# A dilated 3x3 convolution: the tile framework's streams replaced by hand-written ones, with a loop on TensorE

## The chip, the cores and the metric

The kernel runs on one core of a Trainium2 chip. The metric is the device time of one execution in microseconds (us). A core has TensorE (PE in the profile; PEld is its weight loads), VectorE (DVE), ScalarE (ACT), GpSimd (POOL) and SyncE (SP). Here SP issues every transfer, and 16 DMA engines carry them.

## The reference

```python
batch, c_in, h, w, c_out, k, dilation = 16, 64, 64, 64, 128, 3, 2
x_pad = np.pad(x, ((0, 0), (0, 0), (2, 2), (2, 2)))
for b, co, ci, kh, kw:   # five nested loops
    output[b, co] += weight[co, ci, kh, kw] * x_pad[b, ci, 2*kh : 2*kh + h, 2*kw : 2*kw + w]
```

Everything is float32: the input is 16 images of 64 channels and 64x64 pixels (16.8 MB), the output 16 images of 128 channels (33.6 MB).

## The kernel before

**Tiling.** Two images stand side by side on the 128 partitions (64 channels each), so there are 8 pairs. A pair is cut into 4 groups of 16 rows: 32 groups, numbered G. A matmul multiplies the 64 channels of one image with one tap; the two images use the upper and the lower half of the rows of TensorE's array, so their matmuls stand in twos that run side by side.

**Arithmetic.** The vertical taps are rearranged so that 5 products replace 6 per two output rows. ScalarE casts a pair's chunk to 16 bits (`cast`, L74). VectorE adds rows that lie two apart (`rowsum`, L86). TensorE makes three sums in PSUM for each group: psP from the row sums (weights of kind 0, 6 matmuls), psA (kinds 1 and 2, 12 matmuls) and psB (kinds 3 and 4, 12 matmuls), all at L172. ScalarE copies psP to SBUF (`p_sb`, L234). VectorE adds p_sb to psA and to psB and writes two rows of the output in turn (L241). psP has one buffer of two PSUM banks, psA and psB share three.

**Head.** SP loads the weights (L89) and then x (L65): pair 0 in two parts, pair 1, pair 2. The weights are combined into the 5 kinds on VectorE, ScalarE and GpSimd (L112 to L116) and turned by matmuls with an identity (L125), with dummy matmuls (L102) between.

**Order of the work.** The kernel is written in the order in which each engine is to work, inside `tc.manual_schedule()`; the tile framework places the waits. Every matmul of all 32 groups is an instruction of its own, with a weight load ahead of it. For each group the order is: products (P, A, B; in group 0 A, B, P), copy of psP, up to two casts for later groups (`casts`), the row sum of the next group, the two additions. SP's queue holds loads and stores in one fixed order (end of the loop over G): after pair 0's halves come `store_both` (L192) and the loads of pairs 3 and 4, after pairs 1 and 2 `store` (L186) mixed with the loads of pairs 5, 6 and 7, and then stores alone. x has three float32 buffers, the output three (each two images, 4.2 MB). The transfers' completions are counted on eight semaphores used in turn, so that a transfer also waits for the one eight before it.

**End.** The last pair is stored in halves. The last 8 rows of one first half (`ROWS4`, `FOUR`) are split into 124 partitions and 4 partitions. The second halves of the last two images (1 MB each) go out after group 31. L310 is the end of the program, which waits for all transfers and lets the engines meet.

Of the kernel before, what the change touches and what calls it, by code (L numbers as in the profile page):

```python
# [10 lines left out]
def kernel(  # L11
# [7 lines left out]
    nc = tc.nc  # L19
# [5 lines left out]
    assert B % 2 == 0  # L25
# [15 lines left out]
    ngroups = npairs * NG  # L41
    chunk_rows = [(g * GR + (d if g else 0), min((g + 1) * GR + d, H)) for g in range(NG)]
    XF = 3

    wpool = ctx.enter_context(tc.tile_pool(name="wpool", bufs=1))
    fpool = ctx.enter_context(tc.tile_pool(name="fpool", bufs=XF))
    xpool = ctx.enter_context(tc.tile_pool(name="xpool", bufs=3))
    sxpool = ctx.enter_context(tc.tile_pool(name="sxpool", bufs=2))
    opool = ctx.enter_context(tc.tile_pool(name="opool", bufs=3))
    spool = ctx.enter_context(tc.tile_pool(name="spool", bufs=3))  # L50
    ppool = ctx.enter_context(tc.tile_pool(name="ppool", bufs=1, space=bass.MemoryType.PSUM))
    apool = ctx.enter_context(tc.tile_pool(name="apool", bufs=3, space=bass.MemoryType.PSUM))
# [4 lines left out]
    ctx.enter_context(tc.manual_schedule())  # L57

    x32_tiles, x16_tiles, xs_tiles, o_tiles = {}, {}, {}, {}

    def load(pb, cuts=(0, H)):
        if pb not in x32_tiles:
            x32_tiles[pb] = fpool.tile([P, HW], f32, tag="x32", name="x32")
        for lo, hi in zip(cuts[:-1], cuts[1:]):
            nc.sync.dma_start(  # L65
                out=x32_tiles[pb][:, lo * W : hi * W], in_=x_pair[pb, :, lo * W : hi * W]
            )

    def cast(c):
        pb, g = divmod(c, NG)  # L70
        lo, hi = chunk_rows[g]
        if g == 0:
            x16_tiles[pb] = xpool.tile([P, HW], f16, tag="x16", name="x16")
        nc.scalar.copy(  # L74
            out=x16_tiles[pb][:, lo * W : hi * W], in_=x32_tiles[pb][:, lo * W : hi * W]
        )

    def rowsum(c):
        pb, g = divmod(c, NG)
        if g == 0:  # L80
            xs_tiles[pb] = sxpool.tile([P, HW // 2], f16, tag="xs", name="xs")
        v = x16_tiles[pb][:, g * GR * W : (g + 1) * GR * W].rearrange(
            "p (b e q) -> p b e q", e=2, q=2 * W
        )
        s = xs_tiles[pb][:, g * NH : (g + 1) * NH].rearrange("p (b q) -> p b q", q=2 * W)
        nc.vector.tensor_tensor(out=s, in0=v[:, :, 0], in1=v[:, :, 1], op=add)  # L86

    w32 = wpool.tile([CO, CI * KH * KW], f32, name="w32")
    nc.sync.dma_start(out=w32, in_=weight.rearrange("o i h w -> o (i h w)"))  # L89
    load(0, (0, 2 * GR + d, H))  # L90
    load(1)
    load(2)
    zero = wpool.tile([P, 512], f16, name="zero")
    nc.vector.memset(zero, 0.0)  # L94
    ident = wpool.tile([P, P], f16, name="ident")
    make_identity(nc, ident)

    dm = ppool.tile([P, 2 * NH], f32, tag="p", name="dm")

    def dummies(n):  # L100
        for _ in range(n):
            nc.tensor.matmul(out=dm[:, 0:512], lhsT=zero[:, 0:P], rhs=zero)  # L102

    KINDS = 5
    NT = KINDS * KW
    wd = wpool.tile([CO, NT * CI], f16, name="wd")
    wdv = wd.rearrange("o (k j i) -> o k j i", k=KINDS, j=KW)
    wv = w32.rearrange("o (i h w) -> o h w i", h=KH, w=KW)
    w_sb = wpool.tile([P, NT * CO], f16, name="w_sb")

    dummies(8)
    nc.vector.tensor_copy(out=wdv[:, 0], in_=wv[:, 1])  # L112
    nc.gpsimd.tensor_tensor(out=wdv[:, 3], in0=wv[:, 0], in1=wv[:, 1], op=sub)  # L113
    nc.scalar.copy(out=wdv[:, 2], in_=wv[:, 0])  # L114
    nc.vector.tensor_tensor(out=wdv[:, 1], in0=wv[:, 2], in1=wv[:, 1], op=sub)
    nc.gpsimd.tensor_copy(out=wdv[:, 4], in_=wv[:, 2])  # L116

    wts = [apool.tile([P, 1024], f32, tag="ab", name="wt") for _ in range(3)]

    def turn(k):  # L120
        c0 = k // 3 * 512
        for j in range(KW):
            t = k * KW + j
            for r in range(2):
                nc.tensor.matmul(  # L125
                    out=wts[k % 3][r * CI : (r + 1) * CI, c0 + j * CO : c0 + (j + 1) * CO],
                    lhsT=wd[:, t * CI : (t + 1) * CI],
                    rhs=ident,
                )
        return w_sb[:, k * KW * CO : (k + 1) * KW * CO], wts[k % 3][:, c0 : c0 + KW * CO]  # L130

    x16_tiles[0] = xpool.tile([P, HW], f16, tag="x16", name="x16")
    t0 = turn(0)
    dummies(2)
    nc.vector.tensor_copy(out=t0[0], in_=t0[1])  # L135
    t1 = turn(1)
    nc.scalar.copy(out=t1[0], in_=t1[1])  # L137
    t2 = turn(2)
    nc.vector.tensor_copy(out=t2[0], in_=t2[1])  # L139
    dummies(1)  # L140
    t3 = turn(3)
    t4 = turn(4)
    dummies(1)
    nc.vector.tensor_copy(
        out=x16_tiles[0][:, 8 * W : 18 * W], in_=x32_tiles[0][:, 8 * W : 18 * W]
    )
    nc.scalar.copy(out=x16_tiles[0][:, 0 : 8 * W], in_=x32_tiles[0][:, 0 : 8 * W])
    nc.scalar.copy(out=t3[0], in_=t3[1])
    nc.vector.tensor_copy(out=t4[0], in_=t4[1])
    rowsum(0)  # L150

    ahead = [1]

    def casts(G):
        for n in range(2 if G else 3):
            c = ahead[0]
            if c >= ngroups or c > G + (7 if c < 2 * NG else 5):
                return
            cast(c)
            ahead[0] += 1  # L160

    def product(ps, src, kind, blk0, nblk, first, last):
        for j in (1, 0, 2):
            dw = (j - 1) * d
            o0, o1 = max(0, -dw), W - max(0, dw)
            t = kind * KW + j
            for hb in range(2):
                pp = slice(hb * CI, (hb + 1) * CI)
                rhs = src(pp, dw + o0, dw + o1)
                po = ps[:, hb * NH + blk0 * 2 * W : hb * NH + (blk0 + nblk) * 2 * W]  # L170
                po = po.rearrange("p (r w) -> p r w", w=W)[:, :, o0:o1]
                nc.tensor.matmul(  # L172
                    out=po,
                    lhsT=w_sb[pp, t * CO : (t + 1) * CO],
                    rhs=rhs,
                    start=first and j == 1,
                    stop=last and j == 2,
                )

    def blocks(x16, b0, n, e):  # L180
        v = x16.rearrange("p (b e r w) -> p b e r w", e=2, r=2, w=W)
        return lambda pp, c0, c1: v[pp, b0 : b0 + n, e, :, c0:c1]

    def store(pb, m, r0=0, r1=H, rows=((0, P),)):
        for lo, hi in rows:
            nc.sync.dma_start(  # L186
                out=out_img[2 * pb + m, lo:hi, r0 * W : r1 * W],
                in_=o_tiles[pb][lo:hi, m * HW + r0 * W : m * HW + r1 * W],
            )

    def store_both(pb, r0, r1):
        nc.sync.dma_start(  # L192
            out=out_img[2 * pb : 2 * pb + 2, :, r0 * W : r1 * W].rearrange("m o q -> o m q"),
            in_=o_tiles[pb].rearrange("p (m q) -> p m q", m=2)[:, :, r0 * W : r1 * W],
        )

    FOUR = ((0, P - 4), (P - 4, P))
    ROWS4 = 8

    for G in range(ngroups):  # L200
        pb, g = divmod(G, NG)
        x16 = x16_tiles[pb]
        xs = xs_tiles[pb].rearrange("p (r w) -> p r w", w=W)
        if g == 0:
            o_tiles[pb] = opool.tile([P, 2 * HW], f32, tag="osb", name="osb")
        o = o_tiles[pb].rearrange("p (m b e q) -> p m b e q", m=2, e=2, q=2 * W)
        b0 = g * NBLK

        def summed():
            ps = ppool.tile([P, 2 * NH], f32, tag="p", name="psP")  # L210
            sv = lambda pp, c0, c1: xs[pp, g * GR // 2 : (g + 1) * GR // 2, c0:c1]
            product(ps, sv, 0, 0, NBLK, True, True)
            return ps

        if G:
            psP = summed()

        psA = apool.tile([P, 2 * NH], f32, tag="ab", name="psA")
        product(psA, blocks(x16, b0, NBLK, 1), 1, 0, NBLK, True, False)
        z = 1 if g == 0 else 0  # L220
        product(psA, blocks(x16, b0 + z - 1, NBLK - z, 1), 2, z, NBLK - z, False, True)

        psB = apool.tile([P, 2 * NH], f32, tag="ab", name="psB")
        product(psB, blocks(x16, b0, NBLK, 0), 3, 0, NBLK, True, False)
# [3 lines left out]
        if not G:  # L228
            psP = summed()
# [85 lines left out]
```

## Time and profile before

| | |
|---|---|
| device time, median of 3 runs (lowest to highest) | 126.77 us (126.62 to 127.77) |
| the profiled execution: its span, first to last instruction | 125.0 us |
| median above that span | 1.8 us |
| TensorE busy | 105.8 us in 2004 instructions (1002 matmuls, 1002 weight loads) |
| VectorE, ScalarE, GpSimd busy | 91.0, 64.9, 2.2 us |
| bytes moved | 50.8 MB, mean 406 GB/s |

The profile gives the span of the profiled execution, and no separate device time of it; the 1.8 us are counted as lying around the span. A line of the waits says which engine waited for whom, how long in total, how often and the longest. In a timeline each row has the start, the length, engine, line and tiles. A row of the table by stretches has the busy time of the engines, the granted clock, the share of the 16 DMA engines' time in use and the GB/s moved.

### The profile page before, as it was taken

Reading aid. Unit: us, or ns where it says so; the run is one execution under the profiler, and the core shown is the slowest. Engines: PE = TensorE matmul, PEld = TensorE weight load, DVE = VectorE, ACT = ScalarE, POOL = GpSimd, SP = SyncE. Lnnn points to the kernel's source line nnn. Section 1 sums busy time; section 2 is a strip of 40 time slices with the busy share of each in tenths; the row PEclk is TensorE's granted clock in tenths of the full one; section 3 lists DMA queues with packets and bytes.
Section 4 is the critical chain, followed back from the end, with each engine's and each line's share of the span. In section 5 each row is a group of like instructions: output and inputs, shape, how many; then the busy total and the mean of one; then the engine's idle time right before and its main releaser. Section 6 shows DMA issues by size and latency. Waiting matters only on the chain.

```text
span 125.0 us, 2343 instructions
## 1 busy us (share of the span) xinstructions
PE 105.8 (85%) x1002; PEld 57.0 (46%) x1002; DVE 91.0 (73%) x103; ACT 64.9 (52%) x68; POOL 2.2 (2%) x8
## 2 busy tenths in 40 slices
PE   6996999999999999999999999999999999600000
PEld 2353555555555555555555555555555555200000
DVE  0561998988898889888988898889888988700000
ACT  4188896665666566656665666566653333100000
POOL 2400000000000000000000000000000000000000
PEclk9999999999999999999999999999999999985555
DMA  5999999999999999999999999999999999999991
GB/s 142 368 450 435 430 401 315 430 422 420 443 427 435 412 441 438 401 435 435 425 430 427 420 435 430 435 420 435 420 430 430 430 425 435 430 414 412 420 395 73
DMA packets 4722, 50.78 MB, mean 406 GB/s; under 512 B 488, under 2 KB 488, under 8 KB 1000
## 3 DMA queue, kind: packets, MB, share of 16 engines
q1 hardware_dynamic: 4712, 50.63, 96.7%
q8 instruction: 8, 0.13, 0.4%
q14 instruction: 2, 0.02, 0.0%
HBM read 17.07 MB, written 33.55 MB: 405 GB/s over the span
## 4 chain that ended last, share of the span: by engine, by line
PE 76%; DMA 6%; ACT 2%; DVE 1%; DVEq 1%; SPq 1%; issue 0%
PE psA L172 31%; PE psB L172 30%; PE psP L172 16%; DMA x<-in_x_dram 6%; ACT x L74 2%; DVE osb L241 1%; DVEq L310 1%; ACT p_sb L234 1%; SPq L65 0%; SPq L89 0%; DVEq L241 0%
## 5 line engine op out<-in xcount | busy, mean ns | idle before, releaser
L172 PEld LDWEIGHTS <-w_sb 64*128 64x128 f16 x960 | 54.6, 94 | 45.8 <-issue 1.4
L234 ACT COPY p_sb<-psP 128x1024 f32<-128x1024 f32 x32 | 32.4, 1012 | 36.9 <-issue 21.5
L241 DVE TENSOR_TENSOR osb<-psA,p_sb 128x1024 f32<-128x1024 f32 x32 | 39.2, 1225 | 13.4 <-PE psA L172 9.8
L172 PE MATMUL psA<-x,w_sb 64*128 64x496 f16 (+3 forms) x384 | 45.1, 365 | 0.0
L172 PE MATMUL psB<-x,w_sb 64*128 64x496 f16 (+3 forms) x384 | 45.1, 365 | 0.0
L241 DVE TENSOR_TENSOR osb<-psB,p_sb 128x1024 f32<-128x1024 f32 x32 | 39.1, 1222 | 0.0
L74 ACT CAST x<-x 128x1024 f16<-128x1024 f32 (+2 forms) x31 | 32.1, 1044 | 0.5 <-DMA x<-in_x_dram 0.3
L172 PE MATMUL psP<-xs,w_sb 64*128 64x496 f16 (+1 forms) x192 | 26.0, 371 | 1.1 <-ACT p_sb L234 1.1
L86 DVE TENSOR_TENSOR xs<-x 128x512 f16<-128x512 f16 x32 | 13.3, 416 | 0.4 <-ACT x L74 0.4
L102 PE MATMUL dm<-zero 128*128 128x512 f16 x12 | 5.3, 579 | 1.2 <-DVE zero L94 1.2
L102 PEld LDWEIGHTS <-zero 128*128 128x128 f16 x12 | 1.4, 128 | 3.2 <-issue 1.8
L112 DVE CAST wd<-w 128x192 f16<-128x192 f32 x1 | 0.5, 503 | 2.4 <-DMA w<-in_weight_dram 2.4
L125 PEld LDWEIGHTS <-wd 128*64 128x64 f16 x30 | 1.0, 118 | 1.8 <-DVE wd L112 0.8
L137 ACT CAST w_sb<-wt 128x384 f16<-128x384 f32 x1 | 0.5, 478 | 2.3 <-PE wt L125 2.3
L114 ACT ACT_TABLE_LOAD x1 | 1.3, 1283 | 0.7 <-PEq L296 0.7
L125 PE MATMUL wt<-ident,wd 128*64 128x128 f16 x30 | 1.6, 241 | 0.0
L114 ACT CAST wd<-w 128x192 f16<-128x192 f32 x1 | 0.5, 539 | 1.5 <-DMA w<-in_weight_dram 1.5
L139 DVE CAST w_sb<-wt 128x384 f16<-128x384 f32 x1 | 0.6, 557 | 0.7 <-PE wt L125 0.7
L135 DVE CAST w_sb<-wt 128x384 f16<-128x384 f32 x1 | 0.6, 558 | 0.5 <-PE wt L125 0.5
L94 DVE MEMSET zero<- 128x256 uint32 x1 | 0.3, 272 | 0.9 <-PEq L296 0.9
L113 POOL TENSOR_TENSOR wd<-w 128x192 f16<-128x192 f32 x1 | 0.8, 799 | 2.3 <-DMA w<-in_weight_dram 2.3
L116 POOL CAST wd<-w 128x192 f16<-128x192 f32 x1 | 0.8, 806 | 0.0
(11 smaller groups left out, 3.8 us busy)
## 6 DMA issues: line engine op xcount, KB each, us to landing
out_dram<-osb SPq DMA_DIRECT2D x13, 2048.0 KB, 14.9
x<-in_x_dram SPq DMA_DIRECT2D x6, 2048.0 KB, 17.0
out_dram<-osb SPq DMA_DIRECT2D x5, 1024.0 KB, 13.1
x<-in_x_dram SPq DMA_DIRECT2D x2, 1024.0 KB, 13.2
x<-in_x_dram SPq DMA_DIRECT2D x1, 1088.0 KB, 5.6
x<-in_x_dram SPq DMA_DIRECT2D x1, 960.0 KB, 7.4
out_dram<-osb SPq DMA_DIRECT2D x1, 768.0 KB, 15.4
w<-in_weight_dram SPq DMA_DIRECT2D x1, 288.0 KB, 2.8
```

The source lines that it names most:

```text
L74: nc.scalar.copy(out=x16_tiles[pb][:, lo * W : hi * W], in_=x32_tiles[pb][:, lo * W : hi * W])
L86: nc.vector.tensor_tensor(out=s, in0=v[:, :, 0], in1=v[:, :, 1], op=add)
L102: nc.tensor.matmul(out=dm[:, 0:512], lhsT=zero[:, 0:P], rhs=zero)
L113: nc.gpsimd.tensor_tensor(out=wdv[:, 3], in0=wv[:, 0], in1=wv[:, 1], op=sub)
L114: nc.scalar.copy(out=wdv[:, 2], in_=wv[:, 0])
L116: nc.gpsimd.tensor_copy(out=wdv[:, 4], in_=wv[:, 2])
L125: nc.tensor.matmul(out=wts[k % 3][r * CI : (r + 1) * CI, c0 + j * CO : c0 + (j + 1) * CO], lhsT=wd[:, t * CI : (t + 1) * CI], rhs=ident,)
L135: nc.vector.tensor_copy(out=t0[0], in_=t0[1])
L172: nc.tensor.matmul(out=po, lhsT=w_sb[pp, t * CO : (t + 1) * CO], rhs=rhs, start=first and j == 1, stop=last and j == 2,)
L234: nc.scalar.copy(out=p_sb, in_=psP)
L241: nc.vector.tensor_tensor(out=o[:, :, b0 : b0 + NBLK, e], in0=ps.rearrange("p (m b q) -> p m b q", m=2, q=2 * W), in1=pv, op=add,)
L310: with _tile.TileContext(nc) as tc:
```

## The change

The framework's tiles and pools are replaced by fixed buffers, one list of work for each engine and semaphores placed by hand. What it does:

- **Streams.** ScalarE's and VectorE's lists keep the order of before, with one semaphore that counts each engine's finished instructions. P, A and B of all groups rotate through four PSUM buffers of two banks. The 16-bit input has two buffers instead of three. Group 0 computes P first, like the others.
- **TensorE loop.** The matmuls of 8 groups (two pairs) are written once and run four times in a `Fori` loop. The loop body holds 240 matmuls with their weight loads; the code ahead of it holds the 42 matmuls of the head. As the body can't wait for values that change with G, GpSimd waits for VectorE's and ScalarE's counts and passes on three tokens for each group (tX: the row sum is there; tP: p_sb is copied; tA: psA is added); TensorE takes one ahead of each of the three sums.
- **Transfers.** Sizes and order are those of before, the split into 124 and 4 partitions among them. Each transfer has a semaphore of its own. The weights, pair 0's two parts and pairs 1 and 2 are issued ahead of the block in which the engines' streams stand. The two last half images are issued behind that block, that is after all engines have met at its end, and the waits for the last three pairs' stores follow.

The core of the new code (removed lines are those of the kernel above):

```diff
+class Line:
+
+
+    def __init__(self, engine, sem):
+        self.e, self.sem, self.n, self.seen = engine, sem, 0, {}
+
+    def after(self, *marks):
+        for sem, value in marks:
+            if self.seen.get(sem.num, 0) < value:
+                self.seen[sem.num] = value
+                self.e.wait_ge(sem, value)
+
+    def did(self, ins):
+        ins.then_inc(self.sem, 1)
+        self.n += 1
+        return (self.sem, self.n)
...
+    XF, XH, XO, XP = 3, 2, 3, 3
+    AHEAD = 5
...
+        ps = [
+            ctx.enter_context(nc.psum_tensor(f"ps{i}", [P, 2 * NH], f32))[:, :] for i in range(4)
+        ]
...
+        sT = semaphore("turned")
+        sP, sQ, sR = semaphore("prod_p"), semaphore("prod_a"), semaphore("prod_b")
+        tX, tP, tA = semaphore("tok_x"), semaphore("tok_p"), semaphore("tok_a")
+        V, A, G_ = Line(nc.vector, sV), Line(nc.scalar, sA), Line(nc.gpsimd, sG)
...
+        class Move:
+            def __init__(self, out, in_):
+                self.out, self.in_ = out, in_
+                self.sem = semaphore(f"dma{ndma[0]}")
+                ndma[0] += 1
+                self.mark = (self.sem, 16)
...
+        for G in range(ngroups):
+            if not G:
+                casts(0)
+            put_a(("p", G))
+            if G:
+                casts(G)
+            if G + 1 < ngroups:
+                put_v(("sum", G + 1))
+            put_v(("a", G))
+            put_v(("b", G))
...
+        def refill(pb, move):
+            go(move, *(cast_marks(pb - XF, 0) + cast_marks(pb - XF, NG - 1)))
...
+        go(load_w)
+        for pb in range(XF):
+            for _, _, m in loads[pb]:
+                go(m)
+        refill(XF, loads[XF][0][2])
+        go(store_both(0, 0, H // 2), mark_v[("b", 1)])
+        refill(XF, loads[XF][1][2])
+        go(store_both(0, H // 2, H), mark_v[("b", 3)])
+        refill(XF + 1, loads[XF + 1][0][2])
+        done = lambda pb, g: mark_v[("b", pb * NG + g)]
+        go(store(1, 0), done(1, 3))
+        go(store(1, 1, 0, H // 2))
+        refill(XF + 2, loads[XF + 2][0][2])
+        go(store(1, 1, H // 2, H))
+        go(store(2, 0), done(2, 3))
+        refill(XF + 3, loads[XF + 3][0][2])
+        go(store(2, 1))
+        refill(XF + 4, loads[XF + 4][0][2])
+        for pb in range(3, npairs):
+            if pb < npairs - 1:
+                go(store(pb, 0), done(pb, 3))
+                go(store(pb, 1))
+            else:
+                go(store(pb, 0, 0, 2 * GR), done(pb, 1))
+                go(store(pb, 1, 0, 2 * GR - ROWS4))
+                for rows in ((0, P - 4), (P - 4, P)):
+                    go(store(pb, 1, 2 * GR - ROWS4, 2 * GR, rows))
...
+        def slot(G, which):
+            return ps[(3 * G + which) % 4]
+
+        head = 2 + len(loads[0]) + XF - 1 - 1
+        for move, marks in sp[:head]:
+            assert not marks
+            nc.sync.dma_start(out=move.out, in_=move.in_).then_inc(move.sem, 16)
+
+        with nc.Block(no_gpsimd_drain=True) as block:
+
+            @block.sync
+            def _(e):
+                S = Line(e, semaphore("sp"))
+                for move, marks in sp[head:]:
+                    S.after(*marks)
+                    e.dma_start(out=move.out, in_=move.in_).then_inc(move.sem, 16)
+
...
+                G_.after(load_w.mark)
+                G_.did(e.tensor_tensor(out=wdv[:, 3], in0=wv[:, 0], in1=wv[:, 1], op=sub))
+                G_.did(e.tensor_copy(out=wdv[:, 4], in_=wv[:, 2]))
+                G_.after(mark_v["t4"], mark_a["t3"])
+                e.sem_inc(tP, 1)
+                e.sem_inc(tA, 1)
+                G_.after(mark_v[("sum", 0)])
+                e.sem_inc(tX, 1)
+                for G in range(ngroups - 1):
+                    G_.after(mark_v[("sum", G + 1)])
+                    e.sem_inc(tX, 1)
+                    G_.after(mark_a[("p", G)])
+                    e.sem_inc(tP, 1)
+                    G_.after(mark_v[("a", G)])
+                    e.sem_inc(tA, 1)
...
+                    elif key[0] == "cast":
+                        pb, g = divmod(key[1], NG)
+                        lo, hi = chunk_rows[g]
+                        A.after(*loaded(pb, lo, hi))
+                        if pb >= XH:
+                            A.after((sR, (pb - XH) * NG + min(g + 1, NG - 1) + 1))
+                        A.did(
+                            e.copy(
+                                out=x16[pb % XH][:, lo * W : hi * W],
+                                in_=x32[pb % XF][:, lo * W : hi * W],
+                            )
+                        )
+                    else:
+                        G = key[1]
+                        A.after((sP, G + 1))
+                        if G >= XP:
+                            A.after(mark_v[("b", G - XP)])
...
+                e.wait_ge(*mark_v["zero"])
+                dummies(8)
+                e.wait_ge(*mark_v["wd0"])
+                e.wait_ge(sG, 2)
+                turn(0)
...
+                def take(token):
+                    e.wait_ge(token, 1)
+                    e.sem_inc(token, -1)
...
+                def group(G):
+                    pb, g = divmod(G, NG)
+                    x_, b0 = x16[pb % XH], g * NBLK
+                    sv = xs[pb % XH].rearrange("p (r w) -> p r w", w=W)
+                    rows = slice(g * GR // 2, (g + 1) * GR // 2)
+                    take(tX)
+                    summed = lambda pp, c0, c1: sv[pp, rows, c0:c1]
+                    product(slot(G, 0), summed, 0, 0, NBLK, True, True).then_inc(sP, 1)
+                    take(tP)
+                    product(slot(G, 1), blocks(x_, b0, NBLK, 1), 1, 0, NBLK, True, False)
+                    z = 1 if g == 0 else 0
+                    product(
+                        slot(G, 1), blocks(x_, b0 + z - 1, NBLK - z, 1), 2, z, NBLK - z, False, True
+                    ).then_inc(sQ, 1)
+                    take(tA)
+                    product(slot(G, 2), blocks(x_, b0, NBLK, 0), 3, 0, NBLK, True, False)
+                    z = 1 if g == NG - 1 else 0
+                    product(
+                        slot(G, 2), blocks(x_, b0 + 1, NBLK - z, 0), 4, 0, NBLK - z, False, True
+                    ).then_inc(sR, 1)
+
+                with e.Fori(0, npairs // XH):
+                    for G in range(XH * NG):
+                        group(G)
+
+    last = osb[(npairs - 1) % XO]
+    for m in range(2):
+        nc.sync.dma_start(
+            out=out_img[2 * npairs - 2 + m, :, HW // 2 :],
+            in_=last[:, m * HW + HW // 2 : (m + 1) * HW],
+        )
+    with tc.tile_critical(no_gpsimd_drain=True):
+        for pb in range(npairs - XO, npairs):
+            for s in stores[pb]:
+                nc.sync.wait_ge(s.sem, 16)
```

## The prediction

> **What bounds the kernel now.** I read the page first, because its share of engines and its row of transfers tell which of the two is full.
>
> ```profile
> span 125.0 us, 2343 instructions
> PE 105.8 (85%) x1002; PEld 57.0 (46%) x1002; DVE 91.0 (73%) x103; ACT 64.9 (52%) x68; POOL 2.2 (2%) x8
> ...
> DMA  5999999999999999999999999999999999999991
> ...
> q1 hardware_dynamic: 4712, 50.63, 96.7%
> q8 instruction: 8, 0.13, 0.4%
> ...
> w<-in_weight_dram SPq DMA_DIRECT2D x1, 288.0 KB, 2.8
> ```
>
> The transfers fill 96.7% of 16 engines' time; TensorE fills 85%. The chain of waits on the page gives TensorE 76%, but it ends in a VectorE addition and in VectorE's drain at the end of the program, which is only one engine waiting for the others. So I went on to the stretches of the end, with the columns busy time by engine, granted clock, share of the DMA engines, GB/s.
>
> ```profile
> 94.00:100.00 6.00, 6.00 (x62) 3.42 (x60) 5.43 (x7) 2.00 (x3) 0.00 (x0) 1.00 1.00 423
> ...
> 118.00:120.00 2.00, 0.00 (x0) 0.00 (x0) 0.00 (x0) 0.00 (x0) 0.00 (x0) 0.50 1.04 435
> 120.00:122.00 2.00, 0.00 (x0) 0.00 (x0) 0.00 (x0) 0.00 (x0) 0.00 (x0) 0.50 0.84 356
> 122.00:124.00 2.00, 0.00 (x0) 0.00 (x0) 0.00 (x0) 0.00 (x0) 0.00 (x0) 0.50 0.22 94
> ```
>
> The last addition ends at 109.5, and the transfers go on at full rate until 120 and end unevenly by about 124.2. The waits of SP's queue agree: at L310, the program's end, it waits for stores.
>
> ```profile
> SPq L310 <- DMA out_dram<-osb: 13.2, 3, 8.5
> ```
>
> So the end is set by bytes over rate, 50.6 MB at about 430 GB/s, by when the first transfer starts, and by what follows the last. An engine counts only where it is so late that the transfers run dry. That cover is worked out from bytes. After 118 the three rows leave 2.0 + 1.7 + 0.4 = 4.1 us of full use, so with an even end the transfers would be done at 122.1. Pair 6's first store is issued at 97.12 (timeline below), when 8.4 MB are still to be issued, 19.5 us at 430 GB/s: the transfers ahead of it last until 102.6. A transfer starts about 1.1 us after its issue (the first is issued at 0.74, and the stretch from 0 to 2 us has a share of 0.11). Pair 6's store may thus come 4.4 us later at no cost. By the same sum pair 2's store, issued at 47.64, has 4.1 us, and the last two half images, issued at 109.49 with 2.1 MB, have 6.6 us.
>
> **The change, part by part.** Sizes, order and data of the transfers are unchanged, also the 124 and 4 partitions.
>
> *Start.* Ahead of the first transfer SP now signals itself and waits for it once more. The trace has no such step alone. The end of the program has a run of such steps: from the last landing (124.2) to the last instruction (125.0) some eight signals and waits follow each other, 0.1 us each. I take +0.1 (0 to 0.2).
>
> *Group 0.* P comes first, and needs the row sum, done at 8.35, so TensorE starts at about 8.5 instead of 7.70. Before, P of group 1 stood at 11.99 after 1.1 us of waiting for the copy of psP, the only buffer. Now P has another buffer: three sums take 0.63 + 1.27 + 1.27 = 3.2 us, so group 0 ends at 11.7 and group 1's A can follow p_sb's copy at about 12.2 instead of 12.62. On VectorE the first addition waits for p_sb in either order. Bounds -0.4 to +0.9 for the groups (the start of the sum, if nothing is regained), nothing for the end: covered by 4 us of queued transfers.
>
> *Tokens.* Three for each group, through one more engine, so VectorE or ScalarE, then GpSimd, then TensorE. Waiting GpSimd has nothing else queued behind it, but it serves the tokens in order, so a late row sum would hold back p_sb's token too. The timeline of a late group shows the room (start, length, engine):
>
> ```profile
> 97.12 13.45 SPq L186 DMA_DIRECT2D out_dram<-osb  x8
> ...
> 102.64 1.01 ACT L234 COPY p_sb<-psP 128x1024 f32<-128x1024 f32 x1 [2.16 <-PE psP L172]
> 103.10 0.41 DVE L86 TENSOR_TENSOR xs<-x 128x512 f16<-128x512 f16 x1
> ...
> 103.94 1.23 DVE L241 TENSOR_TENSOR osb<-psA,p_sb 128x1024 f32<-128x1024 f32 x1 [0.42 <-PE psA L172]
> 104.92 0.81 PE L172 MATMUL psP<-xs,w_sb 64*128 64x512 f16 x6
> ...
> 105.55 1.45 PE L172 MATMUL psA<-x,w_sb 64*128 64x512 f16 x12
> ...
> 106.82 1.29 PE L172 MATMUL psB<-x,w_sb 64*128 64x512 f16 x12
> ```
>
> The row sum ends at 103.51 and P begins at 104.92: 1.4 us of room. The copy ends at 103.65 and A begins at 105.55: 1.9. The addition ends at 105.17 and B begins at 106.82: 1.65. Two hops of 0.1 to 0.2 us fit in each. The waits themselves cost TensorE between nothing and one exposed weight load (94 ns) each: 72 of them up to pair 6 are 0 to 6.8 us. I take 0, since the rows put the tokens a microsecond ahead, so that the loads can run ahead as they do now. At the upper end pair 6 would be 2.4 us beyond its cover.
>
> *Buffers.* With two 16-bit inputs a cast waits for B of the group seven back, which is long done; the row sums and casts keep their order. SP no longer waits for the transfer eight before; those waits ended earlier than others beside them. Nothing.
>
> *Loop.* TensorE's code was read as it ran: 2004 instructions, 8 packets of 16 KB, one for about 250 instructions, each some 1.0 us of one engine (0.4% of 16 x 125 us, over 8). The body has 8 groups of 60 instructions and 3 waits, some 506, about two packets' worth, and lies on three. If it stays in TensorE's memory, up to six packets fall away: 0.4 us if spread over 16 engines, down to nothing if the engines that end last were not those hit. I take 0, the range -0.5 to 0. If it does not stay, each of three jumps back (ahead of groups 8, 16 and 24) waits for code. The nearest row for a small fetch is the weight load, 2.8 us from issue to landing; with a packet of 1.0 us in a full engine ahead, 3.8. Below, 0. I take 0, since all code is there once by the second run through, and keep 3.8 for the range (rival).
> [...] No jump back stands in this trace.
>
> *End.* The last half images now go out after all engines have met and signalled SP, ten steps of 0.1 or so after 109.49: 1 us, 0.5 to 2, within their cover of 6.6. After the last landing SP has three more steps ahead of the closing ones: +0.3 (0.1 to 0.5).
>
> **Sum.** 125.0 + 0.1 + 0.3 = 125.4 us of span. The profiled execution has a span and no device time of its own; the median of 126.77 stands 1.8 above its span, which I add: 127.2. Its own range is 126.4 to 127.6.
>
> **Rivals.** *Code read again (slower).* At each jump TensorE stands, and pairs 2, 4 and 6 lose one, two and three waits. One wait of 2.8 costs pair 2 nothing (cover 4.1). Three are 8.4 at pair 6, less 4.4 of cover: 4.0 us in which the transfers stand, so 131.2. If the queued matmuls hide 1 us of each, 5.4 - 4.4 = 1.0: 128.2. With 3.8 it is 134.2. I put it at 129.7, between the first two. It decides above 1.5 us for one jump. For it: code came in all along in step with the instructions, so nothing shows that old code is kept. Against it: nothing shows that it isn't kept, and the body is a quarter of what ran.
>
> *An even end (faster).* The rows after 118 show 2.1 us between an even end (122.1) and the real one (124.2). If packets of code made the late engines late, their absence brings up to this. Taking 1.8 of it: 127.2 - 1.8 = 125.4. It needs over 1.7 us to be seen as a gain. Against it: the 8 rows of the last pair lie on few engines, and these remain late; 8 packets of 1.0 us on 16 engines are too few to explain all.
>
> *The loop saves nothing and hides nothing*, because transfers bind: that is my forecast.
>
> **Chances.** Forecast 0.50, code read again 0.36, an even end 0.14. A measurement of this kernel can't tell less than about 1% from no change (125.5 to 128.0). Faster by over 1%: 0.10 of the even end and 0.02 of the forecast, 0.12. Slower: 0.33 of the code and 0.02 of the forecast, 0.35. Within 1%: 0.53. The range of 125.8 to 131.0 leaves out the better part of the even end (0.1) and the long waits (0.1).
>
> **What would show it.** Loop: the q8 row, 2 or 3 packets if the code stays, 12 or more if not; and gaps of TensorE ahead of groups 8, 16 and 24, none or 2 to 4 us. Tokens: TensorE's gaps between sums, and psB's last end near 108. Transfers: the DMA row full from 2 to 120 us; a dip after 100 speaks for the rival. Start and end: SP's first issue at about 0.85, and 1.1 us from the last landing to the end. The forecast is wrong if TensorE ends after 113, or if the transfers end evenly.

## The result, and the profile after

The changed kernel takes 128.47 us (median of 6 runs, 127.52 to 130.5) against 126.72 us (126.56 to 127.77) before in the same session: 1.0104 of before, 95% interval 1.0065 to 1.0144. Run once more (e1_again) it takes 128.38 us, 1.0102 [1.0053, 1.0152]. So it is some 1.3 us slower: about 1%, a small loss, but 1 lies outside the interval. The forecast of 127.2 us and its own range up to 127.6 were too low; the wide range held. Ratios and intervals leave out single executions that were disturbed, among them the profiled one of e2_unrolled below (133.9 us of span), so no time is read from that profile.

The profiled execution took 127.52 us, the fastest of the six, with a span of 125.8 us. The page after, first its span, engines, transfers and queues:

```profile
span 125.8 us, 2579 instructions
...
PE 105.5 (84%) x1002; PEld 56.6 (45%) x1002; DVE 90.6 (72%) x103; ACT 64.9 (52%) x68; POOL 2.2 (2%) x8
...
DMA  3999999999999999999999999999999999999971
...
q1 hardware_dynamic: 4712, 50.63, 96.1%
q8 instruction: 2, 0.03, 0.1%
q14 instruction: 3, 0.02, 0.0%
```

The same 4712 packets and 50.63 MB fill the DMA engines from about 2 to 120 us, as before; TensorE is no busier. Two rows have changed: TensorE's code came in 2 packets instead of 8, and the trace holds 2579 instructions instead of 2343, though every engine's count of work (x1002, x103, x68, x8) is that of before. Of the 236 more, 98 are signals and waits of GpSimd and 98 of TensorE, nearly all of them those of the tokens. The rest is 12 more of TensorE, 16 of VectorE and ScalarE, and 12 others: the loop's own steps, waits and drains.

The stretches of the end (columns: stretch, its length, five engines, granted clock, share of the DMA engines, GB/s):

```profile
118.00:120.00 2.00, 0.00 (x0) 0.00 (x0) 0.00 (x0) 0.00 (x0) 0.00 (x0) 0.50 1.04 436
120.00:122.00 2.00, 0.00 (x0) 0.00 (x0) 0.00 (x0) 0.00 (x0) 0.00 (x0) 0.50 0.70 295
122.00:124.00 2.00, 0.00 (x0) 0.00 (x0) 0.00 (x0) 0.00 (x0) 0.00 (x0) 0.50 0.43 180
124.00:126.00 2.00, 0.00 (x0) 0.00 (x0) 0.00 (x0) 0.00 (x0) 0.00 (x0) 0.50 0.00 0
```

All DMA engines are at work until 120, as before, and then they run out more unevenly: from 122 to 124 us 43% of them still move data, where it was 22%. Most of the time to be explained lies here: in some engines that end late.

**Loop.** The timeline of TensorE where the loop jumps back for the first time (group 8 begins at 34.23; start, length, engine):

```profile
32.70 1.71 PE L420 MATMUL ps<-xh,w_sb 64*128 64x496 f16 x16
34.23 0.81 PE L420 MATMUL ps<-xs,w_sb 64*128 64x512 f16 x6
34.86 2.56 PE L420 MATMUL ps<-xh,w_sb 64*128 64x512 f16 x24
```

The matmuls of group 8 follow those of group 7 without a gap (no wait stands in brackets), and q8 has two packets. So the code is not read again at the jumps; the rival *code read again* is wrong. The answer of waits says the same of the whole run:

```profile
PE ps L420 <- PEq L409: 1.7, 2, 1.5
```

TensorE waits twice for a token, 1.7 us in all, and both times are in the first two groups:

```profile
8.97 0.81 PE L420 MATMUL ps<-xs,w_sb 64*128 64x512 f16 x6 [1.53 <-PEq L409]
9.60 2.56 PE L420 MATMUL ps<-xh,w_sb 64*128 64x512 f16 x24
11.98 0.81 PE L420 MATMUL ps<-xs,w_sb 64*128 64x512 f16 x6
12.95 1.24 PE L420 MATMUL ps<-xh,w_sb 64*128 64x512 f16 x10 [0.16 <-PEq L409]
```

In the first of the two the row sum ends at 8.36 + 0.42 = 8.78 and P begins at 8.97: the way through GpSimd took 0.19 us there.

**Tokens.** In a late group they have the room that the prediction read from the trace of before: the row sum ends at 103.62 + 0.41 = 104.03 and P begins at 105.43, 1.4 us later. The copy ends at 104.12, A begins at 106.07.

```profile
103.11 1.01 ACT L319 COPY psb<-ps 128x1024 f32<-128x1024 f32 x1 [2.16 <-PE ps L420]
103.62 0.41 DVE L351 TENSOR_TENSOR xs<-xh 128x512 f16<-128x512 f16 x1
...
105.43 0.81 PE L420 MATMUL ps<-xs,w_sb 64*128 64x512 f16 x6
...
106.07 2.56 PE L420 MATMUL ps<-xh,w_sb 64*128 64x512 f16 x24
```

**Start and end.** SP's first transfer is issued at 1.01 us instead of 0.74, and the last two half images at 110.69 instead of 109.49:

```profile
1.01 0.38 SPq L247 DMA_DIRECT2D w<-in_weight_dram  x1
...
110.69 1.59 SPq L460 DMA_DIRECT2D out_dram<-osb  x2
```

From the last landing to the last instruction it is 1.24 us (124.52 to 125.76) where it was 0.83 (124.14 to 124.97).

**The late engines.** The trace has the time of every packet and landing, but not the number of the DMA engine; an engine shows as a chain of packets, each of which starts where the last one ends. Two facts carry the rest. First, one of the 16 engines is slow: in the stores, from the first one until the engines stop at about 110 us, its 16 KB packets take 646 ns in the kernel before (mean from 76 to 106 us) where those of all others take 611 ns. It falls behind by about 0.3 us with each store of 2 MB (8 of its packets). In the loads between them it is not slow: from 59.5 to 63.5 and from 69.5 to 73 us, while it carries the loads of pairs 6 and 7, no run of packets above 620 ns stands in the kernel before or after. Second, the split of the 8 rows puts 31 packets of 2 KB (84 ns each, 2.6 us) on each of four engines, and nothing on the other twelve. In the kernel before these two meet: the last of the four lands at 124.14, the slow one at 123.93. In the changed kernel the slow one is last (124.52), and the last of the four lands at 124.38.

### The profile page after: what moved, and what is told of

It is laid out like the page before. It is cut to its first block, busy times and chain, and to the rows that moved or that the text cites. A ratio compares the mean times of both kernels' runs of the same rounds, so it can differ in the third digit from the quotient of the medians.

```text
span 125.8 us, 2579 instructions
## 1 busy us (share of the span) xinstructions
PE 105.5 (84%) x1002; PEld 56.6 (45%) x1002; DVE 90.6 (72%) x103; ACT 64.9 (52%) x68; POOL 2.2 (2%) x8
## 3 DMA queue, kind: packets, MB, share of 16 engines
q1 hardware_dynamic: 4712, 50.63, 96.1%
## 4 chain that ended last, share of the span: by engine, by line
PE 75%; DVE 1%; DVEq 1%; issue 0%
PE ps L420 75%; DVE osb L360 1%; DVEq L249 1%; DVEq L19 0%
## 5 line engine op out<-in xcount | busy, mean ns | idle before, releaser
L360 DVE TENSOR_TENSOR osb<-ps,psb 128x1024 f32<-128x1024 f32 x64 | 76.5, 1222 | 13.8 <-PE ps L420 10.2
L420 PE MATMUL ps<-xh,w_sb 64*128 64x496 f16 (+3 forms) x768 | 84.4, 365 | 0.2 <-PEq L409 0.2
L420 PEld LDWEIGHTS ps<-xh,w_sb 64*128 64x128 f16 x768 | 43.6, 94 | 36.2 <-issue 0.9
L319 ACT COPY psb<-ps 128x1024 f32<-128x1024 f32 x32 | 32.4, 1012 | 35.7 <-PE ps L420 35.6
L309 ACT CAST xh<-xf 128x1024 f16<-128x1024 f32 (+2 forms) x31 | 32.1, 1044 | 1.6 <-DMA xf<-in_x_dram 1.6
L420 PE MATMUL ps<-xs,w_sb 64*128 64x496 f16 (+1 forms) x192 | 26.0, 371 | 1.5 <-PEq L409 1.5
L420 PEld LDWEIGHTS ps<-xs,w_sb 64*128 64x128 f16 x192 | 10.8, 94 | 10.5 <-issue 2.3
L351 DVE TENSOR_TENSOR xs<-xh 128x512 f16<-128x512 f16 x32 | 13.3, 416 | 0.7 <-ACT xh L309 0.7
L374 PE MATMUL ps<-zero 128*128 128x512 f16 x12 | 5.0, 549 | 1.5 <-DVE zero L325 1.5
L334 DVE CAST w_sb<-ps 128x384 f16<-128x384 f32 x3 | 1.7, 556 | 0.5 <-PE ps L381 0.4
```

What stands on the lines that cost most here:

```text
L309: e.copy(out=x16[pb % XH][:, lo * W : hi * W], in_=x32[pb % XF][:, lo * W : hi * W],)
L319: A.did(e.copy(out=psb[G % XP], in_=slot(G, 0)))
L334: V.did(e.tensor_copy(out=o, in_=i))
L351: V.did(e.tensor_tensor(out=s, in0=v[:, :, 0], in1=v[:, :, 1], op=add))
L360: e.tensor_tensor(out=o[:, :, g * NBLK : (g + 1) * NBLK, which], in0=slot(G, which + 1).rearrange("p (m b q) -> p m b q", m=2, q=2 * W), i ...
L374: e.matmul(out=ps[3][:, 0:512], lhsT=zero[:, 0:P], rhs=zero)
```

## The experiments

"Late" below is the last landing; the kernel before has it at 124.14, the changed kernel at 124.52.

**Is it the change at all?** e1_again is the changed kernel as it is.

> The changed kernel once more, for a second profile. Steps theory (signals ahead of the first and behind the last transfer cost a fixed 0.7 us): ratio to before 1.005 to 1.010 and the same 0.25 us later first issue and 1.2 to 1.3 us from the last landing to the end. Uneven-engines theory (some DMA engines fall behind by a different amount in each execution): the time lies anywhere from 127.5 to 129, and the stretch in which the last engines work alone differs from that of the first profile.

1.0102 [1.0053, 1.0152]; its profiled execution lies nearer to the median (128.53 us, span 126.8). First landing of the last transfer 121.02 (before: 120.72), last 125.53.

**The loop.** e2_unrolled:

```
-                with e.Fori(0, npairs // XH):
-                    for G in range(XH * NG):
-                        group(G)
+                for G in range(ngroups):
+                    group(G)
```

> The loop on TensorE undone: all 32 groups written out, tokens and everything else kept. Forecast of the prediction (the loop neither saves nor costs): within 0.3 us of the changed kernel, with 8 packets of code instead of 2. If the jumps back cost: faster than the changed kernel by 0.5 us or more. If the saved packets of code help: slower by 0.3 to 0.5 us.

1.0101 [1.0049, 1.0153], and the code comes in 8 packets again:

```profile
q8 instruction: 8, 0.13, 0.3%
```

As far as the intervals tell, the loop neither costs nor saves anything.

**The late issue of the last half images.** e3_inside:

```
+                go(store(pb, 0, 2 * GR, H), done(pb, 3))
+                go(store(pb, 1, 2 * GR, H))
...
-    last = osb[(npairs - 1) % XO]
-    for m in range(2):
-        nc.sync.dma_start(...)
```

> The two last half images go back into SP's list inside the block, issued when group 31 is added, about 109.5 instead of 110.7. Cover theory (4 to 6 us of queued transfers stand ahead): no change of the landings, time within 0.2 us of the changed kernel, at most 0.1 us off the steps at the end. Rival (the late issue is what makes the end late): 0.5 to 1.2 us faster.

They are issued at 109.29 again, and nothing is gained: 1.0112 [1.0074, 1.0149], late 125.02, between the 124.52 and 125.53 of the changed kernel's two profiles. The 1.2 us are covered, as predicted. From the last landing to the end it is 1.47 us here, 0.23 more than in the changed kernel, so the half images inside the block cost a little at the end.

**The split of the 8 rows.** e4_nosplit:

```
-                go(store(pb, 1, 0, 2 * GR - ROWS4))
-                for rows in ((0, P - 4), (P - 4, P)):
-                    go(store(pb, 1, 2 * GR - ROWS4, 2 * GR, rows))
+                go(store(pb, 1, 0, 2 * GR))
```

> The 8 rows of the last pair are no longer split into 124 and 4 partitions, the half image goes as one transfer over all engines. If the four engines of the split are the late ones in the changed kernel too: faster by 0.5 to 1.5 us and a more even end. If others are late (those that fell behind at the loads): slower by 0.3 to 0.7 us, as each of the others gets 14 KB, 0.5 us, more.

1.0123 [1.0079, 1.0167]: no difference that can be told from the changed kernel. But the landings of the last transfer are plainer without the split. In us behind the first: 13 engines lie between 0 and 0.8, then come 2.13, 3.04 and 4.38. The last is the slow one, which still falls behind from store to store (3.24, 3.55, 3.88 and so on); the other two were set back earlier and keep their distance.

**The tokens.** e5_direct lets TensorE wait for VectorE and ScalarE directly, which needs the loop written out, and takes GpSimd's loop away:

```
-                G_.after(mark_v["t4"], mark_a["t3"])
-                e.sem_inc(tP, 1)
...
-                    take(tX)
+                    T.after(mark_v[("sum", G)], *([] if G else [mark_v["t4"], mark_a["t3"]]))
...
-                    take(tP)
+                    T.after(*([mark_a[("p", G - 1)]] if G else []))
...
-                    take(tA)
+                    if G:
+                        T.after(mark_v[("a", G - 1)])
```

> Tokens undone (and with them the loop, which can't wait for values that change): TensorE waits for VectorE's and ScalarE's counts in its matmuls, GpSimd passes nothing on. Some 190 sequencer instructions fewer. Slow-engine theory (one DMA engine loses about 2.5 ns of transfer for every instruction that any engine runs, and that engine lands last): 0.5 us faster than the changed kernel, ratio to before near 1.006, and the last 16 KB packets of the slow engine at 33 instead of 38 ns over the others. Steps theory (only the steps ahead of and behind the transfers count): no change, ratio near 1.010.

1.0063 [1.0036, 1.009], 128.0 us: the loss falls from 1.0% to 0.6%. The interval overlaps that of the changed kernel, which begins at 1.0065, but five measurements with the tokens (after, e1, e2, e3, and e7 below) all lie between 1.0099 and 1.0112. The trace has 2379 instructions, and the slow engine's packets are back at 644.5 ns (650.1 in the changed kernel).

**Does it grow with the instructions?** e6_sem18 adds 18 signals a group on GpSimd, on a semaphore that nobody waits for, and e7_nop18 18 empty instructions (`e.nop(nofuse=True)`) in the same place:

```
                     G_.after(mark_v[("a", G)])
                     e.sem_inc(tA, 1)
+                    for _ in range(18):
+                        e.sem_inc(tD, 1)
```

> 18 more semaphore increments on GpSimd in each of 31 groups, behind the token of psA, on a semaphore that nobody waits for: 558 more instructions, nothing else. Slow-engine theory: that engine loses 1.4 us more, the time rises by 1 to 1.4 us over the changed kernel (129.5 to 130). Steps theory: no change (128.4).

> The same with 18 empty instructions that touch no semaphore. If the instructions themselves burden the slow engine: as with the 18 increments. If the semaphore traffic does: no change against the changed kernel.

e6_sem18: 1.0241 [1.0188, 1.0295], 130.06 us, 1.7 more than the changed kernel, though TensorE waits no longer than there. e7_nop18: 1.0099 [1.0064, 1.0134], nothing more. The page of e6_sem18 and its stretches:

```profile
span 129.6 us, 3137 instructions
...
q14 instruction: 7, 0.06, 0.1%
```

```profile
124.00:126.00 2.00, 0.00 (x0) 0.00 (x0) 0.00 (x0) 0.00 (x0) 0.00 (x0) 0.50 0.14 57
126.00:128.00 2.00, 0.00 (x0) 0.00 (x0) 0.00 (x0) 0.00 (x0) 0.00 (x0) 0.50 0.06 25
```

0.14 of 16 engines is about two engines, 0.06 is one: they still move data when the others have long been done. The page of e7_nop18:

```profile
span 126.6 us, 2579 instructions
...
q14 instruction: 3, 0.02, 0.1%
```

Its trace has as many instructions as the changed kernel's, and GpSimd's code (q14) came in 3 packets as there, where 558 instructions more brought 7. So the empty instructions were not in the program that ran; e7_nop18 is the changed kernel once more, and says nothing on empty instructions.

e9_mem18 asks whether the semaphores are needed: 18 memsets of one element in the same place, without any semaphore.

```
+                    for i in range(18):
+                        e.memset(spare[0:1, 18 * G + i : 18 * G + i + 1], 0.0)
```

> The changed kernel with 18 memsets of one element in each of 31 groups on GpSimd, behind the addition's token, without any semaphore (558 more instructions, about as many as the 558 semaphore increments of e6_sem18, which cost 1.7 us). Theory A (any instruction that leaves a record slows one DMA engine by about 2.5 ns): 558 x 2.5 ns = 1.4 us more than the changed kernel, 129.8 to 130.2, last landing near 127. Theory B (it is the semaphore changes that slow the engine): no more than the changed kernel, 128.4 +- 0.3, last landing near 125.

130.56 us, 1.0279 [1.0235, 1.0324]. So no semaphore is needed: small instructions do it without them. (Whether their records in the trace, their code or the instructions themselves do it, this run does not separate.) The page (POOL is GpSimd):

```profile
span 129.3 us, 3137 instructions
...
PE 106.1 (82%) x1002; PEld 52.5 (41%) x1002; DVE 90.5 (70%) x103; ACT 64.9 (50%) x68; POOL 22.8 (18%) x566
```

**The split again.** In e6_sem18 and e9_mem18 one of the four engines of the 8 rows is late as well. It lands the 8 rows at 123.59 and 123.31, the other three by 119.9, and it is the last of all at 128.38 and 128.10, while the slow one lands at 126.53 and 126.38. So the times of these two runs hold more than the slow engine's share. e12_mem18_nosplit is e9_mem18 with e4_nosplit's edit.

> e9_mem18 (18 memsets a group more on GpSimd) with the 8 rows of the last pair not split into 124 and 4 partitions, as in e4_nosplit. By the landings of e9_mem18 and e6_sem18, GpSimd's extra instructions make a second DMA engine late, one of the four that take the 8 rows, so that the split puts 2.6 us more on a late engine (last landing 128.1; the other late engine 126.4). Theory: without the split that engine ends 2.0 us earlier and all others 0.6 later, last landing 127.0, 1.1 us faster than e9_mem18: 129.4, 1.019 of before. Rival (the late engine is not one of the four, and the split helps as it did in e4_nosplit's comparison, by 0 to 0.4 us): 130.6 to 131.0, 1.028 or more.

129.9 us, 1.0222 [1.0174, 1.027], 1.5 us less in span, last landing 126.65 for 128.10:

```profile
124.00:126.00 2.00, 0.00 (x0) 0.00 (x0) 0.00 (x0) 0.00 (x0) 0.00 (x0) 0.50 0.13 53
126.00:128.00 2.00, 0.00 (x0) 0.00 (x0) 0.00 (x0) 0.00 (x0) 0.00 (x0) 0.50 0.00 0
```

The landings bear the theory out (127.0 was forecast for the last one). The time is between the two forecasts, and its interval overlaps e9_mem18's, so as a time it is weak evidence. Against e4_nosplit, which differs by the memsets alone, it is clear: 1.0222 [1.0174, 1.027] against 1.0123 [1.0079, 1.0167], some 1.25 us, and in both the slow engine is the last one.

What made that second engine late can be read in part. The last two of GpSimd's 7 code packets came at 78.86 and 98.71 us (e6_sem18), 79.29 and 98.53 (e9_mem18), 78.49 and 97.12 (e12_mem18_nosplit). In each of these six cases one engine, the same both times, falls back by some 0.5 us within the store then under way: 0.31 us for the code packet, and a 16 KB packet that starts where it ends and takes 0.70 to 0.75 us instead of 0.61. The more than 2.5 us by which this engine was behind before that are open.

**Two tries at a better balance, both on the kernel before.** e8_before_k15 stores one half image in 120 and 8 partitions, to spare one engine; e11_direct_rows12 has 16 rows on the four engines instead of 8:

```
-                store(pb, 0, (g - 1) * GR, (g + 1) * GR)
                 if g == 1:
+                    store(pb, 0, 0, 2 * GR, ((0, P - 8), (P - 8, P)))
...
-    ROWS4 = 8
+    ROWS4 = 16
```

> The kernel before, with the last pair's first half image of 1 MB cut into 120 partitions and 8 instead of sent whole, as 124 and 4 put their rows on few engines. If 120 partitions go over 15 engines and the slow engine is the one left out, it is relieved of 64 KB, 2.4 us, and the end comes 0.3 to 0.8 us earlier (126.0). If the slow one is another: the same or up to 0.3 us later.

> The kernel before with 16 instead of 8 rows of the last pair on the lowest four engines (one constant; the label's name is of an earlier plan). By the landings of before, the four engines of the 8 rows end among the first, 3 us ahead of the last one. With 16 rows each of the other engines has 8 rows' share less, 0.6 us, and the four some 1.7 us more, which brings them to 122.4 to 123.3. Theory (late engines are others than the four): last landing 123.5 instead of 124.1, 126.2, 0.995 of before. Rival (the four are late too, or the order is another one each time): same or slower, 126.8 to 128.

Both theories failed. e8_before_k15: 1.0181 [1.0132, 1.023]. The 120 partitions did go to 15 engines and one was spared, but it was an ordinary one, which now ended first; and the 8 KB packets from 98 us on took 136.8 us of engine time together instead of 118.7. Why they became slower is not settled. e11_direct_rows12: 1.0224 [1.0181, 1.0267]. My working had left out that the two half images still follow the 8 rows on the four engines (2 x 2.46 us). (That the four are the lowest ones is not shown: the trace has no engine numbers.) The four were therefore not early in the kernel before but among the last, at 123.25 to 124.14. With 31 packets of 4 KB (160 ns each, 5.0 us instead of 2.6) they end at 124.95 to 126.90 (the last one 1.3 us behind the third), while the slow engine ends at 123.83:

```profile
122.00:124.00 2.00, 0.00 (x0) 0.00 (x0) 0.00 (x0) 0.00 (x0) 0.00 (x0) 0.50 0.30 127
124.00:126.00 2.00, 0.00 (x0) 0.00 (x0) 0.00 (x0) 0.00 (x0) 0.00 (x0) 0.50 0.15 61
126.00:128.00 2.00, 0.00 (x0) 0.00 (x0) 0.00 (x0) 0.00 (x0) 0.00 (x0) 0.50 0.01 4
```

So of the two numbers tried there 8 rows are the better: with them the last of the four and the slow engine end within 0.2 us of each other.

**Tokens and half images together.** e10_direct_inside is e5_direct with e3_inside's edit.

> The changed kernel with TensorE waiting directly on VectorE and ScalarE (no tokens, loop written out) and with the last two half images in SP's list of the block. The accounting theory (0.5 us from the tokens, 0.3 from the later start, 0.4 from the steps behind the last landing, nothing from the place of the half images): 127.9 to 128.0 as with e5_direct, and a landing-to-end stretch of still 1.2 to 1.5 us. Rival (the late half images cost something once the tokens are gone): 127.5 or less.

128.94 us, 1.0115 [1.0071, 1.016]: neither forecast. As a time this run does not bear out the gain of e5_direct. Its runs fall in two heaps, 127.8 to 128.0, where the accounting put them, and 128.9 to 129.2. The profiled one (128.97) is of the upper heap, and its trace shows where its end comes from: the slow engine is not the last one, another is, set back by 1.4 us within one store (the landings of that store, 106.66 to 111.79, spread over 5.13 us, those of the store before over 3.69). One of TensorE's 8 code packets came within it, at 108.78 us, and took 0.93 us; where it ends a 16 KB packet starts that takes 1.01 us instead of 0.61. Together that is 1.3 us. That it was the same engine is read from the times alone. The slow engine's own packets take 645.4 ns, much as without tokens in e5_direct.

**What one entry costs.** The trace has an entry for every instruction and one for every change of a semaphore (a signal leaves two, a memset one). The table sets the slow engine's 16 KB packets that start between 76 and 106 us, 45 to 47 in each kernel but e2_unrolled, against the entries of these 30 us; the packets of all others take 611 ns.

| kernel | instructions in the trace | entries from 76 to 106 us | slow engine, ns | time above 611 for one entry, ns |
|---|---|---|---|---|
| before, e8, e11 | 2343, 2344, 2343 | 826 to 829 | 645.9 to 646.2 | 1.97 to 1.99 |
| no tokens (e5, e10) | 2379, 2378 | 817, 823 | 644.5, 645.4 | 1.92, 1.96 |
| changed (after, e1, e3, e4, e7) | 2576 to 2579 | 937 to 946 | 650.0 to 650.5 | 1.92 to 1.96 |
| 18 signals more a group (e6) | 3137 | 1249 | 662.8 | 1.89 |
| 18 memsets more a group (e9, e12) | 3137, 3134 | 1108, 1121 | 659.3, 660.7 | 2.00, 2.03 |

In the kernel before, 827 entries on 46.7 packets (one starts every 642 ns) are 17.7 for each packet, and 35 ns over 17.7 entries are 2.0 ns for one. In e6_sem18 it is 27 entries for each packet and still 1.9 ns. So the time that the slow engine loses in its stores grows in proportion to the entries: over the range measured here, 17 to 27 for each packet, they fit all of its slowness and not only what the tokens add.

## Why the prediction was right and where it was wrong

- *What binds*: right. TensorE ends at 108.6, the transfers go on at full rate to 120, and neither the loop nor 1.2 us of later issue moves the end. (Of the covers, pair 2's was misadded: 29.4 MB from its store on are 68.3 us at 430 GB/s, which leaves 5.1 us and not 4.1. Nothing else changes by it.)
- *Loop*: right at 0. 2 packets (q8) instead of 8, no gap at the jump (34.23), and e2_unrolled is the same (1.0101 against 1.0104). The body ran four times and 2 packets came in all, so its code was not fetched again. That it would not be was the author's estimate, and how long a body may be before it is, no run shows: none has a loop longer than this one of some 506 instructions.
- *Group 0*: P began at 8.97, not 8.5, and A of group 1 at 12.95, not 12.2. It was 0.33 us later than before, inside the bounds, and covered.
- *Start*: mis-sized, +0.27 us, not +0.1 (at most 0.2). There are two steps, a signal (0.79) and a wait (0.86), and then 0.15 to the transfer.
- *End*: mis-sized, 0.41 us more behind the last landing, not 0.3 (1.24 us in both profiles of the changed kernel, 0.83 before). The late half images cost nothing (e3_inside).
- *Tokens*: this step failed. It asked only whether TensorE waits for them, and there 0 is right: two waits in the first two groups, none later. But the term was not 0. Their instructions slow one DMA engine, from 646.0 ns a packet before (644.5 without tokens in e5_direct) to 650.1. It has some 100 such packets (those of 8 KB counted as half), so by this estimate it ends 0.4 to 0.6 us later, and it is one of those that end last. In after, e1, e3 and e4 it is the last one, but in after by only 0.14 us, so how much of it reaches the end differs from one execution to the next. As a time it rests on e5_direct, which takes the tokens away and stands at 1.0063 against 1.0104, 0.5 us, and e10_direct_inside does not repeat it. That instructions nobody waits for lengthen the run is shown by e12_mem18_nosplit against e4_nosplit: 10.5 ns more a packet, some 1.05 us on 100 packets, and 1.25 us measured.
- *The sum*: 0.27 + 0.41 + 0.5 = 1.2 us, against 1.0104 x 126.72 - 126.72 = 1.3 us measured. With e5_direct 0.7 are left, against 0.8 measured. The single profiled executions scatter by more than these terms (late 124.5 to 125.5 for the same kernel), so the split of 1.3 is an estimate, good to some 0.3 us at best.
- *The wide range*: it held because it had been drawn for the two rivals, and both fell. That the time lies in it is no merit of the sum.
- *An even end*: this rival fell. With 6 of 8 code packets gone, the spread of the last landings was 3.80 us instead of 3.42. Its counter-argument, that the 8 rows' few engines would remain late, was right. A code packet does set an engine back, by 1.3 us and not by 1.0: in the kernel before, each of the last three took some 0.96 us, and the 16 KB packet that starts at its end took 0.98 to 0.99 us instead of 0.61. But the engines that these three hit are not among those that land last. The other half of the spread was in the trace of before already, in the packets of 646 ns, which the prediction did not use.

## What to carry to other kernels

The transfers bound here, and the end was set by the DMA engine that ended last (its landing at 124.52 us in the changed kernel, the last instruction at 125.76). So where transfers bind, read the landings and packet times of single engines, and not only their mean share; the uneven end is room that no faster compute engine will find (in the kernel before 2.1 us, by the prediction's estimate of an even end). An instruction that nothing waits for was still not free here: by the estimate above, some 200 signals and waits cost the slow engine half a microsecond, in executions that were traced. This loop, with two packets of code in all, cost nothing at its jumps (1.0104 against 1.0101 with the loop written out), but saved nothing either, because in the kernel before the engines that the late code packets hit did not end last.

## What was not expected of the hardware

One DMA engine of 16 takes 646 ns for a 16 KB packet of a store instead of 611 while the engines work, and the difference is 1.9 to 2.0 ns for each instruction and each change of a semaphore that the trace records, in all 13 kernels of the table. In the loads (no run of packets above 620 ns) and after the engines have stopped (in the kernel before 54 packets of 16 KB, of all engines, start after 110 us, the longest takes 614 ns) the difference is gone. By what way an entry slows this engine, no run shows. Nor does any run show whether the engine would be slow without the recording: every execution here was one from which a span was taken. So the half microsecond of the tokens may be a cost of being traced; that is a guess from the proportion to the entries. Which of the 16 engines it is, and why a second one was already late in e6_sem18 and e9_mem18 before its code packets came, is open too. No version was found that beats the kernel before; the nearest is e5_direct.
